# A hybrid scan and attention layer: norm sums of the scan one chunk on, one pair's transposes behind the values, and up-stage transposes ahead of two output products

## Chip, cores and metric

The kernel runs on one core of a Trainium2 chip. The metric is the device time of one execution in microseconds (us); a comparison uses the median of several runs. The engines are named as in the profile: PE does the matmuls and the transposes, DVE, ACT and POOL do elementwise work, SP and POOL issue most transfers. Each engine takes its instructions strictly in the order in which they stand in its queue as the traces here show them.

## The reference

One layer over 512 tokens of width 1024, all in float32:

```python
h = rms_norm(x, norm_mix_w)
z, xbc, dt, q, k, v, f = split(h @ w_in)
# scan (SSD): 16 heads of 64 in 2 groups, state 128, 4 chunks of 128 tokens
xs, B, C = split(silu(conv4(xbc)));  dt = softplus(dt + bias)
y = scan(xs * dt, B, C, exp(cumsum(dt * a))) + d * xs
yg = y * silu(z)
y_ssd = yg * rsqrt(mean(yg * yg over the group's 512 columns) + eps) * norm_w
# forgetting attention (FoX): 16 heads of 64, causal
p = softmax(rms_norm(q) @ rms_norm(k).T / 8 + cum[query] - cum[key])
y_fox = p @ v
x = x + concat(y_ssd, y_fox) @ w_out
hf = rms_norm(x, norm_ffn_w)
g, u = split(conv3(hf @ w_up));  x = x + (silu(g) * u) @ w_down
```

## The kernel before

A float32 product is made of three matmuls of float32r operands, each operand being split into a high part (a cast on ACT, names ending in h) and a rest (a subtraction on DVE, names ending in l). `mm3` at L110 issues the three, so one line carries most of PE's rows. `wh` and `wl` are the split halves of a weight block (L96 and L97, folded with a gain at L101 and L102, in the up stage at L898). PE's results go to PSUM banks: four for the mixers' small tiles (`mbank`), one for the output products (`obank`), three for the projections (`bank`).

The work comes in this order. Projections of z, x, B, C (tile `g`) run as a stream of matmuls, and the scan of group 0 is laid among them; then projections of q, k, v (tile `pw`), and the output products (`po`, `out_proj`) of group 0 with the scan of group 1 among them; then the attention of 16 heads in 8 pairs, with further projections and output products as fillers among the heads (`fill`); at last the gated MLP, up and then down.

- The scan, `ssd_scan`, has four chunks of 128 tokens. `scores` makes the decay-weighted scores `sc` and the state's weights `ce` (a load `cs_d` into sc, ACT, POOL, and a product with `cb` on DVE); `chunk` makes `y` on PE in two groups of matmuls on 64 columns each, `y<-sc,x_tok` and, from the second chunk on, `y<-ce,state`; `gated` multiplies with the gate `gz`, splits into `msh` and `msl`, squares into `yt` (ACT), halves yt by two additions on POOL (L524), and sums its 128 columns with a matmul against ones into `ss` (L526), from which `rs`, the norm's factor, comes. `rs` is needed when an output product of that group is added into x (`out_add`, L280).
- The heads: `fox_qk` of a pair transposes the normed q and k (`qkT<-ident,tok`, L581; `tok` is normed with `ms` at L557), then scores `S` (L631 and L632), `prob` on DVE and ACT, `turn` for the transposes `pT` (L654), copies to `pt` on ACT (L656), and for the pair the values `o<-pt,v` (`fox_values`, L664), whose result is split into `mfh` (L672) and `mfl` for the output products of the last four of eight weight blocks.
- The up stage begins with the output products of the last pair of heads by blocks of 128 tokens (`out_part` with `w7`), after each a norm (`up_norm`, L824 and L829) and eight transposes (`up_turn`, `hT<-ident,xw`, L839), whose copies `uh` and `ul` (L842 to L844) and the weights (L898) feed the first product `G`.

The order on each engine is not the order in which the code is written. A scheduler plans all instructions by simulated durations; `urgent()` gives priority, `tc.issue_after(x)` puts an instruction behind x in the plan, and `tc.keep_in_program_order` ties an instruction to the one written before it. So a rule added at one place can move work at others. The fillers among the heads are issued by this loop:

```python
    for n in range(16):
        for f in fillers.get(n, ()):
            fill(f)
        if n % 2 == 0 and n < 14:
            start_pair(n // 2 + 1)
        turn(n)
        if n % 2:
            end_pair(n // 2)
        if n + 2 < 16:
            start_head(n + 2)
```

Of the kernel before, what the change touches and what calls it, by code (L numbers as in the profile page):

```python
# [15 lines left out]
P = 128  # L16
# [23 lines left out]
def tile_hybrid_layer(  # L40
# [243 lines left out]
    def out_proj(pairs, m, halves=(0, 1), scale=None):  # L284
        for half in halves:
            ws = [out_weights(pair, half) for pair in pairs]
            banks = {}
            for t0 in (0, 2):
                for n, (h, l) in enumerate(ws):
                    for tb in (t0, t0 + 1):  # L290
                        s = slice(tb * P, (tb + 1) * P)
                        if n == 0:
                            banks[tb] = bank("po")
                        for j in range(2):
                            k = 2 * n + j
                            c = slice(j * 512, (j + 1) * 512)
                            mm3(
                                banks[tb], m[k][0][:, s], m[k][1][:, s], h[:, c], l[:, c],
                                k == 0, k == 2 * len(pairs) - 1,
                            )  # L300
                        if n == len(ws) - 1:
                            out_add(tb, half, banks[tb], scale)

# [143 lines left out]
    def per_head(ap):  # L447
        return ap[:, :, None].broadcast_to([P, HPG, HD])

    def ssd_scan(g, x_tok, bT, cT, b_tok, gz, dx):  # L450
        mh = pa.tile([P, 4, SEQ], F32R, tag="msh", name="msh")
        ml = pa.tile([P, 4, SEQ], F32R, tag="msl", name="msl")
        hs = slice(g * HPG, (g + 1) * HPG)

        def scores(c):
            s = slice(c * P, (c + 1) * P)
            sc = pss.tile([P, HPG, P], F32, tag="sc", name="sc", bufs=2)
            nc.sync.dma_start(sc, cs_d[None, c * 32 + g * HPG : c * 32 + (g + 1) * HPG, :].to_broadcast([P, HPG, P]))
            last = sc[:, :, P - 1]
            xt = heads(x_tok[c])  # L460
            pool.tensor_tensor(out=xt, in0=xt, in1=per_head(tokS[:, 0, c, hs]), op=ALU.mult)
            dte = ce = None
            if c < NTB - 1:
                dte = dtes[:, (3 * g + c) % 4]
                dve.tensor_sub(dte[:, 0, :], last, tokS[:, 1, c, hs])
                dve.tensor_copy(dte[:, 1, :], last)
                act.activation(dte, dte, AF.Exp)
            if c > 0:
                ce = pss.tile([P, HPG, P], F32, tag="ce", name="ce", bufs=1)
                act.activation(ce, sc, AF.Exp)  # L470
                pool.tensor_tensor(out=ce, in0=ce, in1=cT[:, None, s].broadcast_to([P, HPG, P]), op=ALU.mult)
            pool.affine_select(
                out=sc, in_=sc, pattern=[[0, HPG], [1, P]], compare_op=ALU.is_ge, fill=NEG, base=0,
                channel_multiplier=-1,
            )
            for h in range(HPG):
                act.activation(sc[:, h, :], sc[:, h, :], AF.Exp, bias=nacs[:, c, g * HPG + h : g * HPG + h + 1])
            cb = mbank("cb")
            pe.matmul(cb[:, :P], bT[:, s], cT[:, s], start=True, stop=True)
            dve.tensor_mul(sc, sc, cb[:, None, :P].broadcast_to([P, HPG, P]))  # L480
            return sc, ce, dte

        def side_by_side(o, w, m, start, stop):
            for j in range(4):
                for i, rows in ((1, HI), (0, LO)):
                    h = 2 * j + i
                    ins = pe.matmul(
                        o[rows, j * P : (j + 1) * P], w[:, h * HD : (h + 1) * HD], m[:, h, :],
                        start=start and j == 0, stop=stop and j == 3, skip_group_check=True,
                    )  # L490
                    if (j, i) != (0, 1):
                        tc.keep_in_program_order(ins)

        def chunk(c, state, sc, ce, dte):
            s = slice(c * P, (c + 1) * P)
            o = mbank("y")
            side_by_side(o, x_tok[c], sc, True, c == 0)
            if c > 0:
                side_by_side(o, state, ce, False, True)
            if c < NTB - 1:  # L500
                xt = heads(x_tok[c])
                dve.tensor_mul(xt, xt, per_head(dte[:, 0, :]))
                st = mbank("st")
                pe.matmul(st, b_tok[:, c, :], x_tok[c], start=True, stop=True)
                new = pss.tile([P, 512], F32, tag="state", name="state", bufs=2)
                if state is None:
                    dve.tensor_copy(new, st)
                else:
                    pool.tensor_tensor(out=heads(new), in0=heads(state), in1=per_head(dte[:, 1, :]), op=ALU.mult)
                    dve.tensor_add(new, st, new)  # L510
                state = new
            y = tmp("y", "y").rearrange("p (j f) -> p j f", j=4)
            dve.tensor_add(y, o.rearrange("p (j f) -> p j f", j=4), dx[:, :, s])
            return y, state

        def gated(c, y):
            s = slice(c * P, (c + 1) * P)
            dve.tensor_mul(y, y, gz[:, :, s])
            act.copy(mh[:, :, s], y)
            t = tmp("yt", "yt")  # L520
            act.activation(t, y.rearrange("p j f -> p (j f)"), AF.Square)
            dve.tensor_sub(ml[:, :, s], y, raw(mh[:, :, s]))
            for n in (256, 128):
                pool.tensor_tensor(out=t[:, 0:n], in0=t[:, 0:n], in1=t[:, n : 2 * n], op=ALU.add)  # L524
            o = mbank("ss")
            pe.matmul(o[:, 0:1], t[:, 0:P], ones[:, 0:1], start=True, stop=True)  # L526
            rsqrt(rs[g][:, c : c + 1], o[:, 0:1], 0.25 / 512, 1)

        state, ahead = None, scores(0)
        for c in range(NTB):  # L530
            y, state = chunk(c, state, *ahead)
            if c < NTB - 1:
                ahead = scores(c + 1)
            gated(c, y)
        return [(mh[:, j, :], ml[:, j, :]) for j in range(4)]
# [35 lines left out]

    turned_last = [None]

    def fox_qk(pair, tq, tk):
        qs = [pf.tile([P, SEQ], F32R, tag="qs", name="qs", bufs=4) for _ in range(2)]
        ks = [pf.tile([P, 2, SEQ], F32R, tag="ks", name="ks", bufs=4) for _ in range(2)]
        pr = pair % 2
        for tok, w in ((tk, kw), (tq, qw8)):
            t = mbank("qkT")
            for tb in range(NTB):  # L580
                turned_last[0] = pe.transpose(  # L581
                    t[:, tb * P : (tb + 1) * P], tok[:, tb, pr * P : (pr + 1) * P], ident
                )
            for hd, (own, other) in enumerate(HALVES):
                src, sw = t[own, :], w[own]
                if tok is tq:
# [72 lines left out]
    def fox_values(pair, turned, v):  # L659
        o = obank("o")  # L660
        for kb in range(NTB):
            for i, rows in ((1, HI), (0, LO)):
                pt, w = turned[i][kb]
                ins = pe.matmul(  # L664
                    o[rows, kb * P :], v[:, kb, (2 * pair + i) % 8, :], pt[:, w : w + SEQ - kb * P],
                    start=kb == 0, stop=kb == NTB - 1, skip_group_check=True,
                )
                if (kb, i) != (0, 1):
                    tc.keep_in_program_order(ins)
        mh = pmf.tile([P, SEQ], F32R, tag="mfh", name="mfh", bufs=2)  # L670
        ml = pmf.tile([P, SEQ], F32R, tag="mfl", name="mfl", bufs=2)
        act.copy(mh, o)  # L672
        dve.tensor_sub(ml, o, raw(mh))
        return mh, ml
# [83 lines left out]
# [3 lines that stand above are left out]
        if n % 2 == 0 and n < 14:  # L761
            start_pair(n // 2 + 1)
        turn(n)
        if n % 2:
            end_pair(n // 2)
        if n + 2 < 16:
            start_head(n + 2)
# [54 lines left out]
    def up_norm(tb):  # L822
# [8 lines left out]
            )  # L831
        return ins

    def up_turn(tb, t):
        xw, s = row(tb)
        for c in range(2):
            for j in range(4):
                o = c * 512 + j * P
                pe.transpose(t[:, c, j * P : (j + 1) * P], xw[:, o : o + P], ident)  # L839
        tv = t.rearrange("p c (j f) -> p c j f", j=4)  # L840
        if tb < 2:
            act.copy(oh[:, 0:2, :, s], tv)  # L842
# [415 lines left out]
    for tb in range(NTB):  # L1258
        if tb == 2:
            out_part(wa1[0], m1, 1, (2, 3), rs[1])  # L1260
        out_part(w7[1], mf[6:8], 1, (tb,))
        if tb == NTB - 1:
            weights, tokens = plain(0)
            weights(B12, spare())
            weights(B22)
        out_part(w7[0], mf[6:8], 0, (tb,))
        if tb < NTB - 1:
            with urgent():
                up_norm(tb)
# [332 lines left out]
```

## Time and profile before

| what | us |
|---|---|
| median of three runs (775.80 to 775.88) | 775.82 |
| the profiled execution, its own time | 775.94 |
| its span, first to last instruction | 774.2 |
| PE busy | 759.9 |
| DVE busy | 607.9 |
| ACT busy | 482.0 |
| POOL busy | 226.7 |

The sums are made against the profiled execution, 775.94, which lies 0.12 above the median. PE's busy time is 98% of the span, so about 14.3 us are left in which PE does nothing. A row's duration on PE is not its price: matmuls are pipelined, and the distance from one start to the next is what a row costs. The mean granted clock of PE was 0.999.

### The profile page before, as it was taken

The page shows a single profiled execution, that of the slowest core. Times are in us where ns is not written, and L with a number is a line of the kernel's source. Part 1 is how long each engine was busy: PE and PEld are TensorE (multiplying, and loading weights), DVE is VectorE, ACT ScalarE, POOL GpSimd, SP SyncE. Part 2 cuts the span into 40 slices and gives each one's busy share as a digit, 9 for nine tenths or more (in the row PEclk, how much of TensorE's full clock was granted, in tenths as well). Part 3 has the DMA queues.
Part 4 walks back from the last instruction along what each step waited for, and adds up shares of the span by engine and source line. Part 5 has one row for each costly group of instructions (what it writes and reads, how often), then busy time and mean ns, then how long its engine had stood idle before and what let it go on. Part 6 is the DMA issues. An engine that isn't in the chain of part 4 may idle for free.

```text
span 774.2 us, 12517 instructions
## 1 busy us (share of the span) xinstructions
PE 759.9 (98%) x4647; PEld 651.4 (84%) x4647; DVE 607.9 (79%) x957; ACT 482.0 (62%) x838; POOL 226.7 (29%) x264
## 2 busy tenths in 40 slices
PE   9999999999999999999999999999999999999997
PEld 6888777777888777787777799999999999888785
DVE  5896999777558775578795788888888898998784
ACT  7655657643478776685773566666666666665451
POOL 0001356635351553324200002333333332223120
PEclk9999999999999999999999999999999999999999
DMA  8534323242154142534221317888888878899992
GB/s 336 176 104 141 108 82 110 96 148 70 54 180 134 55 150 57 148 107 139 82 81 55 136 55 145 196 196 194 195 193 194 195 174 198 214 248 209 233 185 84
DMA packets 35293, 113.44 MB, mean 147 GB/s; under 512 B 4192, under 2 KB 5280, under 8 KB 35232
## 3 DMA queue, kind: packets, MB, share of 16 engines
q1 hardware_dynamic: 24464, 75.94, 28.6%
q0 software_dynamic: 10336, 36.18, 25.9%
q8 instruction: 36, 0.59, 0.3%
q10 hardware_dynamic: 432, 0.52, 0.2%
q14 instruction: 25, 0.20, 0.1%
HBM read 106.76 MB, written 2.20 MB: 141 GB/s over the span
## 4 chain that ended last, share of the span: by engine, by line
PE 77%; DVE 8%; issue 5%; DMA 4%; ACT 3%; POOL 2%; SPq 0%; DVEq 0%; POOLq 0%; ACTq 0%
PE G L110 19%; PE pw L110 15%; PE Z L110 10%; PE po L110 10%; PE g L110 5%; PE Y L110 4%; PE o L664 3%; PE pT L654 2%; PE X L110 2%; DVE wl L97 2%; DMA sc<-cs_d 2%; DMA T<-in_wdown_dram 2%; PE j L110 1%; PE S L631 1%; PE S L632 1%
## 5 line engine op out<-in xcount | busy, mean ns | idle before, releaser
L110 PE MATMUL pw<-wl,xh 128*128 128x512 f32 x192 | 75.9, 395 | 0.2 <-DVE wl L97 0.2
L110 PE MATMUL pw<-wh,xh 128*128 128x512 f32 x192 | 75.6, 396 | 0.0
L110 PE MATMUL pw<-wh,xl 128*128 128x512 f32 x192 | 75.4, 395 | 0.0
L97 DVE TENSOR_TENSOR wl<-wraw,wh 128x1024 fp32r<-128x1024 f32 x51 | 66.0, 1295 | 11.6 <-ACT wh L96 11.3
L110 PE MATMUL G<-ul,wh 128*128 128x256 f32 x264 | 72.7, 277 | 0.3 <-DVE ul L844 0.3
L110 PE MATMUL G<-uh,wh 128*128 128x256 f32 x264 | 72.6, 277 | 0.0
L110 PE MATMUL G<-uh,wl 128*128 128x256 f32 x264 | 71.6, 277 | 0.8 <-DVE wl L898 0.8
L96 ACT CAST wh<-wraw 128x1024 fp32r<-128x1024 f32 x51 | 53.4, 1047 | 22.0 <-PE po L110 10.4
L943 POOL DMA_DIRECT2D Ta<-in_wup_dram x30 | 26.3, 875 | 116.5 <-DVE wl L898 113.1
L110 PE MATMUL g<-xh,wh 128*128 128x512 f32 x144 | 57.2, 397 | 0.5 <-ACT wh L188 0.5
L110 PE MATMUL g<-xh,wl 128*128 128x512 f32 x144 | 56.8, 394 | 0.0
L110 PE MATMUL g<-xl,wh 128*128 128x512 f32 x144 | 56.8, 394 | 0.0
L633 DVE CUSTOM_DVE_ANT_0 prob<-S,prob 128x128 f32<-128x128 f32 (+1 forms) x64 | 30.2, 486 | 30.0 <-PE S L632 29.6
L898 DVE TENSOR_TENSOR wl<-Ta,wh 128x1024 fp32r<-128x1024 f32 x40 | 48.7, 1218 | 3.0 <-ACT wh L898 3.0
L637 ACT ACTIVATE prob<-prob,nm 128x128 f32<-128x128 f32 (+1 forms) x64 | 35.8, 560 | 24.1 <-DVE nm L633 24.0
L1189 ACT CAST wh<-T 128x1024 fp32r<-128x1024 f32 (+1 forms) x30 | 29.4, 981 | 34.2 <-DMA T<-in_wdown_dram 20.0
L110 PEld LDWEIGHTS G<-ul,wh 128*128 128x128 f32 x264 | 49.6, 188 | 0.6 <-DVE ul L844 0.5
L110 PEld LDWEIGHTS G<-uh,wh 128*128 128x128 f32 x264 | 49.6, 188 | 0.3 <-ACT wh L898 0.3
L110 PEld LDWEIGHTS G<-uh,wl 128*128 128x128 f32 x264 | 48.9, 188 | 1.0 <-DVE wl L898 1.0
L898 ACT CAST wh<-Ta 128x1024 fp32r<-128x1024 f32 x40 | 42.1, 1053 | 6.7 <-PE Z L110 3.1
L1189 DVE TENSOR_TENSOR wl<-T,wh 128x1024 fp32r<-128x1024 f32 (+1 forms) x30 | 34.0, 1133 | 13.8 <-ACT wh L1189 13.7
L110 PE MATMUL G<-sh,wh 128*128 128x256 f32 x160 | 44.2, 276 | 0.0
(297 smaller groups left out, 2441.5 us busy)
## 6 DMA issues: line engine op xcount, KB each, us to landing
Ta<-in_wup_dram POOLq DMA_DIRECT2D x30, 512.0 KB, 5.5
T<-in_wdown_dram POOLq DMA_DIRECT2D x20, 512.0 KB, 7.6
wraw<-in_wqk_dram SPq DMA_DIRECT2D x16, 512.0 KB, 3.4
wraw<-in_wout_dram SPq DMA_DIRECT2D x16, 512.0 KB, 3.4
wraw<-in_wup_dram SPq DMA_DIRECT2D x14, 512.0 KB, 4.9
wraw<-in_wxbc_dram SPq DMA_DIRECT2D x11, 512.0 KB, 3.4
Ta<-in_wup_dram SPq DMA_DIRECT2D x10, 512.0 KB, 6.9
Tb<-in_wup_dram SPq DMA_DIRECT2D x10, 512.0 KB, 6.2
```

Source lines behind the costliest of these rows:

```text
L96: act.copy(h, r)
L97: dve.tensor_tensor(out=l, in0=r, in1=raw(h), op=ALU.subtract)
L110: ins = pe.matmul(o, a, b, start=start and n == 0, stop=stop and n == 2, **kw)
L631: pe.matmul(sps[:, :n], qst, ks[:, 0, :n], start=True, stop=False)
L632: pe.matmul(sps[:, :n], qst, ks[:, 1, :n], start=False, stop=True)
L633: dve.tensor_tensor_reduce(out=p, in0=sps[:, :n], in1=p, scale=-1.0, scalar=-NEG, op0=ALU.add, op1=ALU.min, accum_out=nm[:, qb : qb + 1],)
L637: act.activation(p, p, AF.Exp, scale=-1.0, bias=nm[:, qb : qb + 1], accum_out=sm[:, qb : qb + 1])
L654: pe.transpose(t[:, w : w + P], prob[:, o : o + P], ident)
L664: ins = pe.matmul(o[rows, kb * P :], v[:, kb, (2 * pair + i) % 8, :], pt[:, w : w + SEQ - kb * P], start=kb == 0, stop=kb == NTB - 1, skip ...
L898: ordered(act.copy(h, r), lambda: dve.tensor_tensor(out=l, in0=r, in1=raw(h), op=SUB))
L943: last_more[0] = nc.gpsimd.dma_start(t, wup[quarter, q], accum_op=ALU.add)
L1189: ordered(act.copy(hs, src[:, :n]), lambda: dve.tensor_tensor(out=ls, in0=src[:, :n], in1=raw(hs), op=SUB))
```

## The change

Three edits, which leave the computation as it is.

1. `gated` no longer issues the sum `ss`. It keeps the squares in a list, and the new `norm_sum(after)` issues the sum behind a given instruction: in chunk c+1 between `y<-sc,x_tok` and `y<-ce,state`; for the last chunk of group 0 behind the first pair of output products; for the last chunk of group 1 behind the first `turn` of the heads (its squares are kept in another buffer).
2. In `fox_qk` the q and k transposes of pair 4 are put behind the last values issued so far in the code, those of pair 2.
3. In the up stage the two output products of token block 2 are put behind the transposes of block 1, and the weights of the up stage's first products are asked for ahead of both products of block 3.

```diff
+    squares = []
+
+    def norm_sum(after):
+        g, c, t = squares.pop(0)
+        o = mbank("ss")
+        with tc.issue_after(after.ins):
+            pe.matmul(o[:, 0:1], t[:, 0:P], ones[:, 0:1], start=True, stop=True)
+        rsqrt(rs[g][:, c : c + 1], o[:, 0:1], 0.25 / 512, 1)
+
@@ out_proj
-                            mm3(
+                            ins = mm3(
...
+                        if squares:
+                            norm_sum(ins)
@@ chunk
-            side_by_side(o, x_tok[c], sc, True, c == 0)
+            own = side_by_side(o, x_tok[c], sc, True, c == 0)
             if c > 0:
+                norm_sum(own)
                 side_by_side(o, state, ce, False, True)
@@ gated
-            t = tmp("yt", "yt")
+            t = pa.tile([P, SEQ], F32, tag="R", name="yt") if g and c == NTB - 1 else tmp("yt", "yt")
...
-            o = mbank("ss")
-            pe.matmul(o[:, 0:1], t[:, 0:P], ones[:, 0:1], start=True, stop=True)
-            rsqrt(rs[g][:, c : c + 1], o[:, 0:1], 0.25 / 512, 1)
+            squares.append((g, c, t))
@@ fox_qk
-                turned_last[0] = pe.transpose(
-                    t[:, tb * P : (tb + 1) * P], tok[:, tb, pr * P : (pr + 1) * P], ident
-                )
+                with tc.issue_after(values_last[-1].ins) if pair == 4 else nullcontext():
+                    turned_last[0] = pe.transpose(
+                        t[:, tb * P : (tb + 1) * P], tok[:, tb, pr * P : (pr + 1) * P], ident
+                    )
@@ fox_values
+        values_last.append(ins)
@@ the loop over heads, behind turn(n)
+        if squares:
+            norm_sum(turned_last[0])
@@ up stage
-        out_part(w7[1], mf[6:8], 1, (tb,))
         if tb == NTB - 1:
             weights, tokens = plain(0)
             weights(B12, spare())
             weights(B22)
-        out_part(w7[0], mf[6:8], 0, (tb,))
+        with tc.issue_after(last_turn[0].ins) if tb == 2 else nullcontext():
+            for half in (1, 0):
+                out_part(w7[half], mf[6:8], half, (tb,))
```

The planner's order changes from the first scan to the up stage. Three places show it. First PE, in the scan of group 0. Before, the sum of chunk 0 stands in the stream of projections, a matmul behind four transposes:

```order
L399 MATMUL xT<-ident,bT 128x128 x4
L110 MATMUL g<-xh,wh 128x512
L526 MATMUL ss<-ones,yt 128x1
L110 MATMUL g<-xl,wh 128x512
L110 MATMUL g<-xh,wl 128x512
```

After, it stands inside the y of chunk 1:

```order
L110 MATMUL g<-xl,wh 128x512
L498 MATMUL y<-sc,x_tok 64x128 x8
L458 MATMUL ss<-ones,yt 128x1
L498 MATMUL y<-ce,state 64x128 x8
L110 MATMUL g<-xh,wl 128x512
```

The sum moved some eighteen matmuls back, from the stream to between the two groups of y. Second, PE at the values of pair 1. Before, transposes of pair 3 (`qkT`) lie between the values of the pair's two heads:

```order
L110 MATMUL pw<-wh,xl 128x512
L664 MATMUL o<-pt,v 64x512
L581 MATMUL qkT<-ident,tok 128x128
L664 MATMUL o<-pt,v 64x512
L581 MATMUL qkT<-ident,tok 128x128
L664 MATMUL o<-pt,v 64x384
L581 MATMUL qkT<-ident,tok 128x128
L664 MATMUL o<-pt,v 64x384
L581 MATMUL qkT<-ident,tok 128x128
L664 MATMUL o<-pt,v 64x256 x2
L664 MATMUL o<-pt,v 64x128 x2
```

After:

```order
L110 MATMUL pw<-wh,xl 128x512
L678 MATMUL o<-pt,v 64x512 x2
L678 MATMUL o<-pt,v 64x384 x2
L678 MATMUL o<-pt,v 64x256 x2
L678 MATMUL o<-pt,v 64x128 x2
L645 MATMUL S<-ks,qs 128x512
L595 MATMUL qkT<-ident,tok 128x128 x5
```

The values stand together and the transposes behind them and a score. Third, DVE in the scan of group 1, where it norms the tokens (`tok`), splits weights (`wl`) and adds output products into x. Before:

```order
L513 TENSOR_TENSOR y<-y,dx 128x512
L557 TENSOR_TENSOR tok<-tok,ms 128x1024
L518 TENSOR_TENSOR y<-y,gz 128x512
L557 TENSOR_TENSOR tok<-tok,ms 128x1024
L97 TENSOR_TENSOR wl<-wraw,wh 128x1024
L510 TENSOR_TENSOR state<-st,state 128x512
L280 SCALAR_TENSOR_TENSOR x_85<-po,misc,x_85 128x512 x2
```

After:

```order
L526 TENSOR_TENSOR y<-y,dx 128x512
L531 TENSOR_TENSOR y<-y,gz 128x512
L476 TENSOR_TENSOR dte<-sc,tokS 128x8
L477 COPY dte<-sc 128x8
L568 TENSOR_TENSOR tok<-tok,ms 128x1024
L97 TENSOR_TENSOR wl<-wraw,wh 128x1024
L280 SCALAR_TENSOR_TENSOR x_85<-po,misc,x_85 128x512
L568 TENSOR_TENSOR tok<-tok,ms 128x1024
```

One addition into x moved ahead of the second `tok`. The second scan itself starts later on PE: `cb` of its first chunk, which stood ahead of the last part of the projections, now stands behind 6 matmuls of the output products, and its first `y` behind 24. Before the last pair's values, PE had ten matmuls of output products behind the transposes `pT` and now has three; behind them it had three ahead of the first that needs their `mfh`, and now none. At the start of the up stage the transposes of blocks 0 and 1 stood between products of blocks 2 and 3 and now stand together ahead of them; on ACT, the square of block 2 now stands ahead of the cast of the weights whose `wl` G's third matmul needs.

More of the change, by code (lines that the diff above doesn't have):

```diff
@@ L492, in side_by_side @@
                         tc.keep_in_program_order(ins)
+            return ins
         def chunk(c, state, sc, ce, dte):
@@ L572, in tile_hybrid_layer @@
     turned_last = [None]
+    values_last = []
     def fox_qk(pair, tq, tk):
@@ L832, in up_norm @@
         return ins
+    last_turn = [None]
     def up_turn(tb, t):
@@ L838, in up_turn @@
                 o = c * 512 + j * P
-                pe.transpose(t[:, c, j * P : (j + 1) * P], xw[:, o : o + P], ident)
+                last_turn[0] = pe.transpose(t[:, c, j * P : (j + 1) * P], xw[:, o : o + P], ident)
         tv = t.rearrange("p c (j f) -> p c j f", j=4)
```

## The prediction

> **What bounds the kernel.** I read the page first, then the waits of the tensor engine (PE), then the timeline of PE at each place the change touches, with the other engines beside it.
>
> ```profile
> span 774.2 us, 12517 instructions
> PE 759.9 (98%) x4647; PEld 651.4 (84%) x4647; DVE 607.9 (79%) x957; ACT 482.0 (62%) x838; POOL 226.7 (29%) x264
> ```
>
> PE is busy 759.9 of 774.2 us, so the end moves only where PE stops, or where its rows take longer than they need. The waits tell the first:
>
> ```profile
> PE ss L526 <- POOL yt L524: 2.0, 2, 1.2
> ...
> PE po L110 <- DVE x L280: 1.4, 1, 1.4
> ...
> PE G L110 <- DVE wl L898: 0.8, 1, 0.8
> ...
> PE G L110 <- DVE ul L844: 0.3, 1, 0.3
> PE po L110 <- DVE x L278: 0.3, 1, 0.3
> ...
> PE pw L110 <- DVE wl L97: 0.2, 1, 0.2
> ```
>
> The columns are the tile and line that waited, who released it, microseconds in total, times, longest. These are the waits in the stretch that the change and the new order touch. What the list cannot show is a row that is merely slow; one such group is below.
>
> **Norm sums (ss).** The matmul needs POOL's two additions of yt, and PE takes its rows in order, so everything behind it stood still twice. Columns: start, duration, engine, line, operation.
>
> ```profile
> 98.72 0.60 PE L399 MATMUL xT<-ident,bT 128*128 128x128 f32 x4
> 99.08 0.47 PE L110 MATMUL g<-xh,wh 128*128 128x512 f32 x1
> 100.72 0.38 PE L526 MATMUL ss<-ones,yt 128*128 128x1 f32 x2 [1.17 <-POOL yt L524]
> ...
> 116.83 0.39 PE L110 MATMUL g<-xl,wh 128*128 128x512 f32 x1
> 118.09 0.38 PE L526 MATMUL ss<-ones,yt 128*128 128x1 f32 x2 [0.88 <-POOL yt L524]
> ...
> 134.20 0.40 PE L110 MATMUL g<-xh,wl 128*128 128x512 f32 x1
> 134.44 0.28 PE L526 MATMUL ss<-ones,yt 128*128 128x1 f32 x2
> 134.58 0.47 PE L110 MATMUL g<-xh,wh 128*128 128x512 f32 x1
> 134.89 0.40 PE L110 MATMUL g<-xl,wh 128*128 128x512 f32 x1
> ```
>
> In the stream a projection matmul starts 0.23 us after the one before (134.20 to 134.44), though its row lasts 0.40; after transposes it is about 0.31 (134.58 to 134.89). So the first stall cost 100.72 − 99.08 − 0.31 = 1.33 us and the second 118.09 − 116.83 − 0.23 = 1.03: together 2.36, some 0.16 each more than the idle shown, since ends overlap. In the changed order a sum stands one chunk on, between the two halves of y. POOL's additions were over at 97.38 + 3.28 and 115.45 + 2.59 in the rows below, and the next y of before starts at 121.28, so the sum never waits there. **Term: −2.36.**
>
> ```profile
> 97.38 3.28 POOL L524 TENSOR_TENSOR yt<-yt 128x256 f32<-128x256 f32 x2 [8.65 <-issue]
> ...
> 115.45 2.59 POOL L524 TENSOR_TENSOR yt<-yt 128x256 f32<-128x256 f32 x2 [1.81 <-ACT yt L521]
> ...
> 118.84 1.21 DVE L480 TENSOR_TENSOR sc<-sc,cb 128x1024 f32<-128x1024 f32 x1
> ...
> 121.28 1.09 PE L487 MATMUL y<-sc,x_tok 128*64 128x128 f32 x16
> 122.20 1.04 PE L487 MATMUL y<-ce,state 128*64 128x128 f32 x16
> 123.17 0.50 PE L110 MATMUL g<-xh,wl 128*128 128x512 f32 x1
> 123.51 0.40 PE L110 MATMUL g<-xh,wh 128*128 128x512 f32 x1
> ```
>
> Part comes back. y of chunk 2 needs sc, which DVE finishes at 118.84 + 1.21 = 120.05. PE stood at this y at 121.28. With 2.36 us less behind it, and one sum shifted in or out, it would stand there at 119.0 to 119.7, while DVE's own chain hardly starts sooner. A wait of 0 to 1.05; I take the end near the later arrival, **+0.35**.
>
> The sum's own price: in the stream 134.44 to 134.58 to 134.89, about 0.14 and 0.08 for the longer row behind it. Inside y it separates two groups that use 64 columns each. From y into the stream one row costs 0.34 us (123.17 to 123.51) against 0.23, so one change of shape is about 0.1. Six sums now lie inside y, each with a change of shape before and behind it that was not there: between 0 and +0.2 each, I take 0.1, the price of one, since what stood behind the sum in the stream (0.08) is saved: **+0.6**. The sum is not hidden by anything, PE being the bound. The Trainium skill (TensorEngine Tiling (Array Packing), Key Properties) states that a change of tiling mode drains TensorE, which speaks against placing a full-width matmul between 64-column ones. The seam at 289.05 to 289.31 further below, 0.26 us for one transpose between such groups, agrees in kind; by it this term would be 6 × (0.26 − 0.09, a transpose among its like) = +1.0 and the sum 0.4 us worse. The two last sums (behind the first pair of output products, and behind the first transposes of the heads) only change place: 0.
>
> **Values of a pair of heads.** Seven of the eight groups of values look like the first row here; one is split.
>
> ```profile
> 259.13 2.38 PE L664 MATMUL o<-pt,v 128*64 128x512 f32 x16
> 261.43 0.50 PE L631 MATMUL S<-ks,qs 128*128 128x512 f32 x1
> ...
> 288.05 1.07 PE L664 MATMUL o<-pt,v 128*64 128x512 f32 x2
> 289.05 0.33 PE L581 MATMUL qkT<-ident,tok 128*128 128x128 f32 x1
> 289.31 1.07 PE L664 MATMUL o<-pt,v 128*64 128x512 f32 x2
> ...
> 292.67 0.87 PE L664 MATMUL o<-pt,v 128*64 128x256 f32 x8
> 293.47 0.50 PE L110 MATMUL pw<-wh,xh 128*128 128x512 f32 x1
> ```
>
> All sixteen together take 261.43 − 259.13 = 2.30 us. The split group takes 293.47 − 288.05 = 5.42 with four transposes in it: two heads that run side by side when adjacent (512 columns of two heads about 1.0) run one after the other (1.0 each, 288.05 and 289.31). No wait shows this, PE being "busy". It is pair 1's values with pair 3's transposes, not the pair that the diff names; but the order of the changed kernel has all eight groups whole, and the four transposes stand with others of their kind, 0.36 us for four (98.72 to 99.08). 5.42 − 2.30 − 0.36 = **−2.7**. What could be late is the scores of pair 3: its transposes come only 2 to 3 us later, and the projection products lie between.
>
> **Two waits that the new order removes.** First pw: DVE's split of the weights (wl, L97) was late by 0.2 because DVE and ACT stood behind the load of sc; in the changed order the cast and the split come ahead of what needs sc. By the same overlap of 0.16: **−0.37**; bounds 0 and −0.37. Second po:
>
> ```profile
> 171.39 5.78 POOL L126 TENSOR_TENSOR ms<-ms,misc 128x16 f32<-128x16 f32 x2 [1.13 <-DVE ms L125]
> ...
> 174.34 1.23 DVE L557 TENSOR_TENSOR tok<-tok,ms 128x1024 f32<-128x1024 f32 x1 [0.49 <-POOL ms L126]
> ...
> 177.21 3.40 DVE L557 TENSOR_TENSOR tok<-tok,ms 128x1024 f32<-128x1024 f32 x1 [1.04 <-POOL ms L126]
> 180.53 2.10 DVE L97 TENSOR_TENSOR wl<-wraw,wh 128x1024 fp32r<-128x1024 f32 x1
> ```
>
> DVE waits for POOL's ms, then two long rows pass before x L280, which frees PE's bank. Now one x L280 stands between the two tok rows, and the second group starts later on PE, its cb and y moved behind 6 and 24 matmuls of output product. So the bank should be free in time: **−1.5** (1.35 idle and the overlap); bounds 0 and −1.5.
>
> **End of the heads.** Before, ten output products lie between the last transposes of prob and the last values; now three. The copies that they cover:
>
> ```profile
> 420.66 1.25 PE L654 MATMUL pT<-ident,prob 128*128 128x128 f32 x10
> ...
> 421.19 1.46 ACT L656 COPY pt<-pT 128x256 f32<-128x256 f32 x3 [3.81 <-PE pT L654]
> ...
> 424.14 2.38 PE L664 MATMUL o<-pt,v 128*64 128x512 f32 x16
> 426.45 0.50 PE L110 MATMUL po<-wh,mfh 128*128 128x512 f32 x1
> ...
> 426.59 0.59 ACT L672 CAST mfh<-o 128x512 fp32r<-128x512 f32 x1 [3.94 <-PE o L664]
> ```
>
> The copies end 421.19 + 1.46 = 422.65; three products end about 422.4, so up to 0.3 of wait. Behind the values the product that needs mfh now follows at once, and mfh is ready 426.59 + 0.59 − 426.45 = 0.73 after them; three products covered that. Bounds 0.2 and 1.0, I take **+0.7**.
>
> **Start of the up stage.** With both transposes ahead of the two output products, ul should come in time (0.3 idle gone), but ACT's order now has a square ahead of the cast of the weights whose wl released G with 0.8 us: the same wl is late by as much or more. Between −1.1 (both waits gone) and +0.4; I take **+0.2**.
>
> **Sum.** −2.36 + 0.35 + 0.6 − 2.7 − 0.37 − 1.5 + 0.7 + 0.2 = −5.1. The whole order from the second scan to the up stage is new, and the planner's durations aren't the chip's: the old order left five waits between 98 and 430 us in the list (2.0 in two, 1.4, 0.3, 0.2), a mean of 0.8. I allow one such in the new one: −4.3. The profiled execution took 775.94 (1.74 around the span) and the runs' median is 775.82, so 771.6 by the one and 771.5 by the other. I forecast **771.5**.
>
> **Rivals.** (1) *Much is given back.* y of chunk 2 waits 1.05, the waits of pw and po stay, the tail costs 1.0, the up stage 0.4, and two new waits of 0.8: −2.36 + 1.05 + 0.6 − 2.7 + 1.0 + 0.4 + 1.6 = −0.4, 775.4: no change. For it speaks that DVE is busy 79% and each of its rows can take two or three times as long beside POOL; against it that the split values are PE's own loss and nothing can return them in place.
>
> (2) *Slower: POOL holds the second scan.* Its chunks start later, so the ms rows (5.78 us for 16 columns, beside DVE) now lie closer ahead of POOL's work on sc and ce for chunk 1, and PE stops at that y. If ms is paid in full there (+5.78) and the po wait stays (+1.5), the sum is −4.3 + 7.3 = +3.0, 778.8; it turns slower than measurable from 5.9 us of added wait on. Against it: some 15 us of output products lie between the y of successive chunks, and its chain took about 10. The Trainium skill (SBUF — State Buffer, Who interferes with whom) states that a VectorE instruction with two SBUF inputs and a GpSimd one that reads SBUF exclude each other for the whole instruction; the 3.40 us tok row agrees, its twin took 1.23 (at 174.34), though POOL was at ms then too: the trace agrees with the first alone.
>
> (3) *Larger gain*: the up stage's waits both go and no new wait comes: −5.1 − 0.2 − 1.1 = −6.4, 769.4.
>
> (4) *The edit does nothing for the pair that it names.* Pair 4's transposes lie behind pair 2's values already; that is so, and costs nothing. Only if the values were split elsewhere would 2.7 be lost: 774.2.
>
> **Chances.** A measurement can tell 0.2%, 1.55 us: below 774.27 is faster, above 777.37 slower. Forecast with its spread (769 to 773.5) 0.58, rival 3 0.08, rival 4 0.10 (near the edge, counted as faster), rival 1 0.16, rival 2 0.08. So faster 0.76, same 0.16, slower 0.08. The range 769.2 to 775.6 leaves out rival 2, the far side of rival 1 and a little below.
>
> **What would show it.** No ss and no wait of ss among PE's waits, unless at y of chunk 2; all eight groups of values at 2.3 us; no wait of pw nor of po on x L280; a new wait of po on mfh near 425, under 1 us; G's wait on wl still there. I am wrong if PE's list shows a y of the second scan waiting for DVE or POOL, or several new waits over 1 us between 150 and 420.

## The result, and the profile after

The changed kernel took 772.19 us (median of four, 770.84 to 772.74) against 775.85: a ratio of 0.995 with an interval of 0.9933 to 0.9967. On a second chip it was 0.9968 (0.9957 to 0.9979). By the medians it is faster by 3.7 us on the first chip and by 2.2 on the second; both intervals leave out 1. The page of the changed kernel, its profiled execution taking 772.68:

```profile
span 770.9 us, 12505 instructions
PE 757.6 (98%) x4647; PEld 651.6 (85%) x4647; DVE 605.1 (78%) x957; ACT 480.8 (62%) x838; POOL 226.5 (29%) x264
```

PE is still busy for all but 13 us. PE's waits in the changed kernel:

```profile
PE y L498 <- DVE sc L491: 1.6, 2, 1.0
...
PE X L110 <- DVE wl L1208: 1.0, 2, 0.8
PE G L110 <- DVE x L278: 0.9, 1, 0.9
...
PE po L110 <- ACT mfh L687: 0.7, 1, 0.7
...
PE G L110 <- DVE wl L917: 0.6, 1, 0.6
PE o L678 <- ACT pt L670: 0.4, 1, 0.4
PE po L110 <- DVE x L278: 0.3, 1, 0.3
```

The waits of ss, of pw and of po on x L280 are gone. In their place stand y on sc, o on pt and po on mfh. Between 140 and 420 us PE's list shows no wait at all.

Where the time went is best read between fixed points that both kernels have: the first y, the first matmul of pw behind the first scan, and G's third matmul. These are the three rows before, and then in the changed kernel:

```profile
87.16 1.09 PE L487 MATMUL y<-sc,x_tok 128*64 128x128 f32 x16
...
140.20 0.39 PE L110 MATMUL pw<-wh,xh 128*128 128x512 f32 x1
...
445.95 0.39 PE L110 MATMUL G<-uh,wl 128*128 128x256 f32 x1 [0.75 <-DVE wl L898]
```

```profile
87.09 1.09 PE L498 MATMUL y<-sc,x_tok 128*64 128x128 f32 x16
...
140.22 0.39 PE L110 MATMUL pw<-wh,xh 128*128 128x512 f32 x1
...
443.22 0.38 PE L110 MATMUL G<-uh,wl 128*128 128x256 f32 x1 [0.56 <-DVE wl L917]
```

So the first scan took 53.13 instead of 53.04, and from there to G 303.00 instead of 305.75. The 2.66 us between the first and the last of these points are the change's own. The two profiles differ by another 0.6 us, most of it in the down stage, which the change does not touch. From its first X to the end this stage took 98.9 to 101.5 us in the profiles here; two profiles of the changed kernel gave 99.6 and 101.0, but 356.13 and 356.24 between the points. From G's third matmul to the first Y, where the down stage begins, it is 208.8 to 209.0 us for every kernel of the table but one, which is told below. I therefore judge each experiment by the distance between the points in its profile, beside its ratio to before as timed on the same chip.

| kernel | first y to pw | pw to G's third | both | timed ratio to before |
|---|---|---|---|---|
| before | 53.04 | 305.75 | 358.79 | 1 |
| changed | 53.13 | 303.00 | 356.13 | 0.995 (0.9933 to 0.9967) |
| changed, second chip | 52.98 | 303.26 | 356.24 | 0.9968 (0.9957 to 0.9979) |
| sums only | 53.04 | 305.98 | 359.02 | 1.000 (0.9983 to 1.0017) |
| up stage only | 53.12 | 306.15 | 359.27 | 1.0005 (0.9994 to 1.0017) |
| sums and pair 4 | 53.04 | 303.75 | 356.79, and 1.4 behind G | 0.9975 (0.9964 to 0.9987) |
| before, values whole | 53.05 | 303.39 | 356.44 | 0.9974 (0.9964 to 0.9985) |
| changed, scores first | 51.17 | 303.28 | 354.45 | 0.9945 (0.9933 to 0.9957) |
| changed, sum behind y | 52.29 | 302.44 | 354.73 | 0.9946 (0.9934 to 0.9958) |
| changed, both of these | 51.55 | 302.47 | 354.02 | 0.9941 (0.9928 to 0.9954) |
| changed, filler later | 52.92 | 302.55 | 355.47 | 0.9949 (0.9934 to 0.9965) |
| scores first, filler later | 51.17 | 302.52 | 353.69 | 0.9925 (0.9911 to 0.9939) |

### The profile page after: what moved, and what is told of

Its sections match the earlier page's. It is cut to its first block, busy times and chain, and to the rows that moved or that the text cites. A ratio compares the mean times of both kernels' runs of the same rounds, so it can differ in the third digit from the quotient of the medians.

```text
span 770.9 us, 12505 instructions
## 1 busy us (share of the span) xinstructions
PE 757.6 (98%) x4647; PEld 651.6 (85%) x4647; DVE 605.1 (78%) x957; ACT 480.8 (62%) x838; POOL 226.5 (29%) x264
## 4 chain that ended last, share of the span: by engine, by line
PE 85%; issue 4%; DMA 4%; DVE 4%; POOL 1%; ACT 1%; SPq 0%; DVEq 0%; POOLq 0%; ACTq 0%
PE G L110 19%; PE pw L110 17%; PE po L110 11%; PE g L110 11%; PE Z L110 10%; PE o L678 2%; DMA T<-in_wdown_dram 2%; PE pT L668 2%; PE Y L110 2%; PE y L498 2%; PE j L110 1%; PE S L645 1%; PE S L646 1%; POOL T L1197 1%; PE qkT L595 1%
## 5 line engine op out<-in xcount | busy, mean ns | idle before, releaser
L110 PE MATMUL G<-sh,wl 128*128 128x256 f32 x160 | 44.2, 277 | 0.0
```

What stands on the lines that cost most here:

```text
L110: ins = pe.matmul(o, a, b, start=start and n == 0, stop=stop and n == 2, **kw)
```

## The experiments

**The edits one by one.** Edit 2 alone was not run: in the trace of before, the transposes of pair 4 (316.85) stand behind pair 2's values (314.20) already. Edit 1 alone is the diff without the parts of `fox_qk`, `fox_values` and the up stage.

> Edit 1 alone (the norm sums one chunk on), the rest as before. In its order the split of a group of values is not gone but has moved: the transposes of pair 4 now lie between the values of pair 2. Theory (two heads of a pair cost 2.3 us when adjacent and 5.4 when split, and edit 2 is there to stop just that): 772.2 + 2.7 = 774.9 us, one group of values at about 5.4 us in the trace, the waits of pw and of po on x L280 gone. Rival (the split costs little because PE would have waited in that place anyway, and the gain is that of the waits): 772.5 us.

Measured: 775.74 us (median of twelve, of which one took 783.14) against 776.04 on that chip, no difference; 359.02 between the points, 0.23 more than before. In its trace the split group is there again, one pair further on, as rows of PE show (pair 2's values, pair 4's transposes):

```profile
315.83 1.07 PE L675 MATMUL o<-pt,v 128*64 128x512 f32 x2
316.83 0.33 PE L592 MATMUL qkT<-ident,tok 128*128 128x128 f32 x1
317.09 1.07 PE L675 MATMUL o<-pt,v 128*64 128x512 f32 x2
...
320.45 0.87 PE L675 MATMUL o<-pt,v 128*64 128x256 f32 x8
321.25 0.33 PE L592 MATMUL qkT<-ident,tok 128*128 128x128 f32 x1
```

From 315.83 to 321.25 are the same 5.42 us as before. The theory's distance, the changed kernel's 356.13 + 2.7 = 358.8, is within 0.2 of the 359.02 measured; the rival's gain is not there. So edit 1 brings nothing alone, and edits 1 and 2 bring 2 us together (356.79, below): the new plan of edit 1 moves the split to the very pair that edit 2 guards.

Edit 3 alone is the part of the diff in the up stage.

> Edit 3 alone (transposes of blocks 0 and 1 ahead of the output products of block 2). The order up to the up stage is that of before, word for word. Theory (G's waits are traded: ul comes in time, but G now waits for the addition into x and still for wl): 775.9 us, within 0.3 of before. Rival (the transposes being earlier, both old waits of G go): 774.7 us.

Measured: 776.53 against 776.04, ratio 1.0005; 0.48 us more between the points. G's waits were traded: it now waits 1.1 for wl and 0.4 for wh, where before it waited 0.8 for wl and 0.3 for ul. The wait for the addition into x, which the theory names, is not in the list; ACT's wh stands in its place. The rival falls.

The change without edit 3:

> The change without edit 3 (the up stage as before). Theory (edit 3 trades waits): 772.2 us, within 0.4 of the change, with G's waits on ul and wl as before. Rival (edit 3 brings about 1 us): 773.3 us.

Measured: 774.17 against 776.04; 356.79 between the points, 0.66 more than the changed kernel, more than the theory's 0.4 and less than the rival's 1. It did not keep the old waits of G: in the new plan G's first matmul waits once, and longer, for DVE, where the last additions into x stand:

```profile
PE G L110 <- DVE misc L125: 2.4, 1, 2.4
```

PE stood still long enough here for its granted clock to fall behind the wait:

```profile
440.00:444.00 4.00, 1.61 (x8) 1.00 0.02 9
444.00:448.00 4.00, 4.00 (x23) 0.57 0.37 131
```

(The columns are PE's busy time and count of matmuls, the granted clock, the DMA share and GB/s.) This cost lies behind the last point: from G's third matmul to the first Y this kernel took 210.3 us, against 208.8 in the changed one. So in these profiles edit 3 is worth nothing alone and 0.7 + 1.4 = 2.1 us in company, since it spares G this long wait. The timed ratios, 0.9975 against 0.9968 and 0.995 on other chips, are too close together to confirm the size, and the profiled execution (776.92) was the slowest of the twelve, so the others may have lost less behind G.

**The largest term by itself.** Before, with one rule more:

```diff
+                with tc.issue_after(values_last[-1].ins) if pair in (3, 4) else nullcontext():
+                    turned_last[0] = pe.transpose(...)
...
+        values_last.append(ins)
```

> Before, with one thing added: the transposes of pairs 3 and 4 are put behind the last values issued so far (pairs 1 and 2). All eight groups of values are then whole; norm sums and up stage as before. Theory (the split is the largest term, 2.7 us, and stands by itself): 773.1 us, with the waits of ss and of po on x L280 still there. Rival (the largest term is the norm sums, and the values were only slow rows in a place with slack): 775.8 us.

Measured: 774.00 against 776.04, ratio 0.9974; 2.35 us less between the points, with the waits of ss (2.1) and of po on x L280 (1.2) still in the list, and a second wait of po on x L278 (0.3) beside them. A rule on two pairs' transposes brings nearly as much as the whole change does.

**What the scan gave back.** In the changed kernel PE, and DVE beside it:

```profile
119.21 0.39 PE L110 MATMUL g<-xh,wl 128*128 128x512 f32 x1
120.14 1.09 PE L498 MATMUL y<-sc,x_tok 128*64 128x128 f32 x16 [0.55 <-DVE sc L491]
...
135.85 0.39 PE L110 MATMUL g<-xh,wh 128*128 128x512 f32 x1
137.29 1.09 PE L498 MATMUL y<-sc,x_tok 128*64 128x128 f32 x16 [1.05 <-DVE sc L491]
```

```profile
116.54 1.22 DVE L535 TENSOR_TENSOR msl<-y,msh 128x512 fp32r<-128x512 f32 x1
...
118.88 1.21 DVE L491 TENSOR_TENSOR sc<-sc,cb 128x1024 f32<-128x1024 f32 x1
...
136.03 1.21 DVE L491 TENSOR_TENSOR sc<-sc,cb 128x1024 f32<-128x1024 f32 x1
```

The product for chunk 3 before:

```profile
134.82 1.21 DVE L480 TENSOR_TENSOR sc<-sc,cb 128x1024 f32<-128x1024 f32 x1
```

DVE's product for chunk 2 stands at 118.88; before, it stood at 118.84. PE could have begun that y at 119.53 (0.32 behind the row ahead, as at other y), 1.75 us earlier than before, and waited. For chunk 3 the product even came 1.2 us later than before. The next kernel moves the split of y behind it:

```diff
-            dve.tensor_sub(ml[:, :, s], y, raw(mh[:, :, s]))
+            with tc.issue_after(weighed[0].ins) if c < NTB - 1 else nullcontext():
+                dve.tensor_sub(ml[:, :, s], y, raw(mh[:, :, s]))
```

(`weighed[0]` is the latest product of sc and cb.) The changed kernel itself was run beside it as the measure:

> The changed kernel again, unedited, as the measure for the other three on this chip, and a second profile of it. Expected 3.7 us less than before on the same chip, with the same waits: y on sc twice (1.6 together), o on pt (0.4), po on mfh (0.7), G twice (1.5); the waits of the down stage (X, Y) may differ.

Measured: 774.11 against 776.33, 2.2 us less and not 3.7; the waits are the same, apart from that of y on sc (1.4 together) and those of the down stage (X 1.5 here).

> The changed kernel with one rule more: DVE's split of y (msl) goes behind the next chunk's product of the scores (sc), so that sc comes some 1.2 us earlier. Theory (the order of DVE's work, not PE's, sets when y of chunks 2 and 3 can start, and it took back what the sums gave): both waits of y on sc go, 1.7 us less than the changed kernel. Rival (sc waits for POOL and ACT just as long, so that the order on DVE does not matter): the waits stay, no difference.

Measured: 771.58, 2.5 us less than the changed kernel beside it; 1.7 to 1.8 less between the points, all of it in the first scan. DVE's sc now comes ahead of the split, and PE's y has no wait:

```profile
116.27 1.20 DVE L493 TENSOR_TENSOR sc<-sc,cb 128x1024 f32<-128x1024 f32 x1
117.39 0.68 DVE L538 TENSOR_TENSOR msl<-y,msh 128x512 fp32r<-128x512 f32 x1
```

```profile
118.36 1.09 PE L500 MATMUL y<-sc,x_tok 128*64 128x128 f32 x16
134.59 1.09 PE L500 MATMUL y<-sc,x_tok 128*64 128x128 f32 x16
```

The theory holds: the gain of the sums was there, and DVE's order withheld it. More than the split moved, though: sc came 2.6 us earlier in chunk 2 and 4.3 in chunk 3, more than the theory's 1.2, because the new plan moved other DVE rows too (`y<-y,dx` from 109.46 to 107.49).

**The sum's place.** `norm_sum` behind the second half of y instead of the first (and the rule of edit 2 for pairs 3 and 4):

> The changed kernel with the sum behind both halves of y instead of between them (and pair 3's transposes also behind the values, so that all groups of values stay whole). Theory (a sum between the halves costs about 0.25 us more than one in the stream, in two changes of shape): y 0.92 and 0.97 us again, 1.3 us less than the changed kernel. Rival (the sum costs what it costs wherever it stands): no difference.

Measured: 772.03, 2.1 less than the changed kernel beside it, 1.4 to 1.5 between the points. First the rows of the changed kernel, then of this one:

```profile
103.76 1.09 PE L498 MATMUL y<-sc,x_tok 128*64 128x128 f32 x16
104.78 0.38 PE L458 MATMUL ss<-ones,yt 128*128 128x1 f32 x2
105.10 1.09 PE L498 MATMUL y<-ce,state 128*64 128x128 f32 x16
106.12 0.50 PE L110 MATMUL g<-xh,wl 128*128 128x512 f32 x1
106.46 0.40 PE L110 MATMUL g<-xh,wh 128*128 128x512 f32 x1
```

```profile
104.26 1.09 PE L498 MATMUL y<-sc,x_tok 128*64 128x128 f32 x16
105.18 1.04 PE L498 MATMUL y<-ce,state 128*64 128x128 f32 x16
106.15 0.38 PE L458 MATMUL ss<-ones,yt 128*128 128x1 f32 x2
106.40 0.48 PE L110 MATMUL g<-xh,wl 128*128 128x512 f32 x1
106.71 0.40 PE L110 MATMUL g<-xh,wh 128*128 128x512 f32 x1
```

2.70 us against 2.45 for the same work: 0.25 for each sum that stands between the halves. The Trainium skill (TensorEngine Tiling (Array Packing), Key Properties) says that a change of tiling mode drains TensorE; the trace agrees that it costs, with this number, but shows no drain as such.

Both together:

> The changed kernel with both: scores ahead of the split of y on DVE, and the sum behind both halves of y. If both theories hold the two gains add: 3.0 us less than the changed kernel. If y still waits for sc, what the sum saves is waited for in the first scan, and the gain is 0.7 us or less.

Measured: 771.82; 2.1 to 2.2 between the points, neither 3.0 nor 0.7. Two waits of y on sc, 0.6 together, are back, and a small one of st (0.2). What the sums save is not the reason, since y starts no earlier behind the first y than in the kernel with the scores first alone (31.6 us in chunk 2, there 31.5). It is sc that comes later, by 0.9 us in chunk 2 and 1.8 in chunk 3, the latter with DVE idle for 2.0 us behind a row of POOL:

```profile
134.61 1.22 DVE L493 TENSOR_TENSOR sc<-sc,cb 128x1024 f32<-128x1024 f32 x1 [2.03 <-POOL yt L539]
```

POOL's own row for that sc ended later as well, 45.6 us behind the first y, there 44.1. Which of the new plan's moves delays it stays open.

**The end of the heads.** One entry of the fillers:

```diff
-    fillers = {..., 13: ["o2"], 15: ["a1"]}
+    fillers = {..., 14: ["o2"], 15: ["a1"]}
```

> The changed kernel with one filler (the output products o2) written one head later. In its order six output products instead of three lie between the last transposes of prob and the last values; behind the values still none ahead of the product that needs mfh. Theory (the two waits at the end of the heads are the price of the missing cover): the wait of o on pt (0.4 idle, 0.5 lost) goes, that of po on mfh (0.7) stays; from the first y to G's third matmul 0.5 us less than the changed kernel. Rival (pt is late for a reason of ACT's own): both stay.

Measured: 772.56 against 776.12; 0.7 less between the points; the wait of o on pt is gone and that of po on mfh stands at 0.71, as the theory has it.

Then one block of group 1's output products moved ahead as well:

```diff
-        if tb == 2:
-            out_part(wa1[0], m1, 1, (2, 3), rs[1])
+        if tb in (0, 2):
+            out_part(wa1[0], m1, 1, (2 + tb // 2,), rs[1])
```

> As the last, and one of the two blocks of group 1's output products moved ahead of the last pair's: then eight products stand ahead of the last values and three between the values and what needs mfh. Theory: both waits at the end of the heads go (1.3 us), but only 12 instead of 24 products are left ahead of the up stage's transposes, whose xw was ready 0.3 us before they started, so these wait up to 2.4 us: slower than the changed kernel by up to 1 us in this stretch. Rival (the transposes have slack): 1.3 us less.

Measured: 781.98 against 776.12, ratio 1.007 (1.0054 to 1.0086), far slower than either theory. Both waits at the end of the heads are gone and the transposes wait, as foreseen, but the theory's sum was 1 us, and the loss beside the kernel before this one is more than 9. The rest is told in the last section. (Its G's third matmul stands behind others, so it has no row in the table.)

The version the experiments point to, scores first and the filler later:

> The changed kernel with the scores ahead of the split of y on DVE, and the filler one head later. If both are separate terms: 1.7 + 0.5 = 2.2 us less than the changed kernel, about 770. Rival (they interact through the new plan): no better than the scores alone.

Measured: 770.13 against 776.12, ratio 0.9925 (0.9911 to 0.9939), and 2.4 to 2.5 less between the points than the changed kernel: the two terms add. It beats the kernel before as timed on this chip; the changed kernel was not run here, and its ratios on two other chips are 0.995 and 0.9968.

## Why the prediction was right, and where its terms were not

The direction, the range and the time (771.5 forecast, 772.19 measured) were right. The sum of the terms was −4.3 us; what the change itself brought between the points is −2.66, little more than half of it. That the median came within 0.7 of the forecast is in part luck: on the second chip the same kernel was only 2.2 us faster than before. Term by term:

| term | forecast | in the runs |
|---|---|---|
| stalls of ss | −2.36 | −2.36, both gone |
| y waits for sc | +0.35 | +1.73, in two chunks |
| sums inside y | +0.6 | +1.5 (6 × 0.25) |
| values whole | −2.7 | −2.35 (alone) |
| wait of pw | −0.37 | gone, with edit 1 alone too |
| wait of po on x L280 | −1.5 | gone, with edit 1 alone too |
| end of the heads | +0.7 | +1.27 |
| start of the up stage | +0.2 | +0.15 |
| one new wait | +0.8 | none from 140 to 420 us |

The sizes in the runs add up to −1.9, against −2.66 between the points. The first scan comes out (−2.36 + 1.73 + 3 × 0.25 = +0.12, measured +0.09); some 0.7 us of gain behind it is in none of these terms. Part of it can be the values, whose −2.35 holds the new wait that came with them.

- **y waits for sc.** The step that failed is "a wait of 0 to 1.05; I take the end near the later arrival". It looked at chunk 2 alone. Chunk 2 lost 120.14 − 119.21 − 0.32 = 0.61 and chunk 3 another 137.29 − 135.85 − 0.32 = 1.12. With the dearer sums, the first scan gained nothing (53.04 and 53.13). This much of rival 1 came true; its waits of pw and po did not.
- **Sums inside y.** "I take 0.1, the price of one" was too low: it was 0.25, above the upper bound of 0.2. The other estimate of the prediction, +1.0 from the seam at 289.05, was nearer and still short.
- **Values.** All eight groups now cost 2.30 us. Right in size: 2.35 when run alone (358.79 − 356.44), and 2.89 from the other side (359.02 − 356.13), with edit 3's part in it. But rival 4's sentence that the rule for pair 4 does nothing, and costs nothing, was read from the order of before. In the order of edit 1 without it, that pair is the one that splits.
- **End of the heads.** The mechanism was right and both waits came, but together they cost 0.49 (421.22 − 420.41 − 0.32) and 0.78, above the bound of 1.0.

```profile
420.41 0.40 PE L110 MATMUL po<-wh,mfl 128*128 128x512 f32 x1
421.22 2.37 PE L678 MATMUL o<-pt,v 128*64 128x512 f32 x16 [0.41 <-ACT pt L670]
424.30 0.50 PE L110 MATMUL po<-wh,mfh 128*128 128x512 f32 x1 [0.71 <-ACT mfh L687]
```

- **Start of the up stage.** G's two waits were replaced by two others, (442.19 − 440.92 − 0.23) + (443.22 − 442.38 − 0.12) = 1.76 us lost against (444.81 − 444.10 − 0.12) + (445.95 − 444.81 − 0.12) = 1.61 before.
- **Rival 2**, POOL holding the second scan, did not come: no y of the second scan waits.

## What to carry to other kernels

Where a scheduler plans the order, an edit is worth what the whole new plan is worth: edits 1 and 3 brought nothing when run alone, the three together brought 2.66 us, and one of the two largest gains came from a pair of heads that none of them names. Look on the busy engine for rows that are longer than their like: the split values were in no list of waits. Before removing a wait, find when the next operand behind it is ready, and shorten that chain too: here one rule for the order on DVE, with what the planner made of it, gave the 1.7 us that the removal had only moved.

## What was not expected of the hardware

The kernel of 781.98 us above showed two things. First, the clock. The transposes hT waited, PE standing still for about 2 us:

```profile
432.77 1.05 PE L858 MATMUL hT<-ident,xw 128*128 128x128 f32 x8
435.77 1.69 PE L858 MATMUL hT<-ident,xw 128*128 128x128 f32 x8 [1.95 <-DVE xw L846]
437.11 0.78 PE L110 MATMUL po<-wh,mfh 128*128 128x512 f32 x1
437.69 0.63 PE L110 MATMUL po<-wl,mfh 128*128 128x512 f32 x1
```

Behind that wait matmuls come 0.43 us apart instead of 0.23, until 439.8; in stretches of 4 us (PE's busy time and count, then the granted clock, the DMA share and GB/s) the clock fell to 0.57:

```profile
432.00:436.00 4.00, 2.05 (x15) 1.00 0.03 9
436.00:440.00 4.00, 4.00 (x15) 0.57 0.74 252
440.00:444.00 4.00, 4.00 (x18) 1.00 0.01 5
```

A wait of 2.2 us thus cost 4.0: 2.2, 0.5 in the slow transposes, 1.3 in six slow matmuls. The clock fell likewise in the change without edit 3, where PE's starts lay 2.8 us apart at the wait for G: from 444.5 to 447.7 its matmuls came 0.21 us apart instead of 0.11. The waits of 1.4 us and less in the other kernels left the clock at 1.00. The Trainium skill (TensorE: Matmul & The Clock Gate, Part 1) lets the clock fall after an idle window of about 3.4 us; here gaps of 2.2 and 2.6 us (2.8 less the usual 0.23) were enough, the second of them between plain matmuls, and the measurement decides.

Second, a pace. At 486.63 us this kernel's G waited 0.5 us for DVE. Up to there its matmuls of 256 columns came 0.1135 us apart, from there on 0.1177, and stayed so for the rest of the up stage. In all other profiles of this study it was 0.1133 to 0.1134 from about 475 to 645 us, and all four timed runs of this kernel lay between 780.25 and 782.67. The two stretches, this kernel first and then the changed one:

```profile
500.00:550.00 50.00, 50.00 (x427) 1.00 0.81 181
```

```profile
500.00:550.00 50.00, 50.00 (x444) 1.00 0.86 194
```

The granted clock is 1.00 in both. Over the 168 us from there to 655 the 4% make some 6.3 us, most of what the kernel lost beside the 4.0. In the changed kernel the pace is as slow from about 456 to 465 us and then comes back. What sets it, and why it does not come back in this kernel, is open: that the wait started it is not shown, and it was not tried by itself.
